# Turning between two sets of accumulation banks, a postponed step and a moved weight sum in the second products of two MLPs

## The chip, the cores and the metric

The kernel runs on one core of a Trainium2 chip. The core has a matrix engine (TensorE, PE in the profile), a vector engine (VectorE, DVE), a scalar engine (ScalarE, ACT), a general engine (GpSimd, POOL) and a queue that issues transfers (SyncE, SP). Matrix products accumulate in eight banks of a memory called PSUM, and VectorE and ScalarE read them out. The metric is the time on the device in microseconds (us), the median of several runs.

## The reference

Two transformer layers on 1024 tokens of width 1024. Layer 0 mixes by sliding-window attention, layer 1 by a gated recurrence (HGRN2); each is followed by an MLP of inner width 4096, and a norm stands before each block and at the end.

```python
def sqrelu_mlp(h, w_up, w_down):
    return jnp.square(jax.nn.relu(h @ w_up)) @ w_down

for layer in range(DEPTH):
    h = rmsnorm(x, mix_norm[layer])
    y = attention(h) if layer % 2 == 0 else hgrn2(h)
    x = x + y
    h = rmsnorm(x, mlp_norm[layer])
    x = x + sqrelu_mlp(h, w_up[layer], w_down[layer])
return rmsnorm(x, final_norm)
```

The change is in the second product of the MLP, `squared @ w_down`: 1024 tokens x 4096 by 4096 x 1024, once in each layer.

## The kernel before

**Precision.** Every float32 operand of a large product is split into a rounded part and the rest (`split`, `weight_split`): a cast on ScalarE or VectorE makes the first (`wh` for weights), a subtraction on VectorE the second (`wl`). One 128x128x512 product is then three matmuls (`mm3`): high by high, high by low, low by high.

**Seven products in place of eight.** `down` cuts both operands into 2x2 blocks and forms the output from seven block products (the Strassen-Winograd scheme), numbered 1 to 7 as in `operands`. Each sums over 16 steps `p`; a step is 12 matmuls, four row blocks `m` times three, and so a product is 192 matmuls. "Pass 6" in this document is `run_pass((6,))`, the 16 steps of product 6; the first pass carries products 1 and 5 step by step together. `T[p]` holds running sums of activations and `S[p]` running sums of weights, both as tiles in on-chip memory; product 5 makes `S[p]`, product 6 uses it, and product 3 needs `a(0, 1) - S[p]`.

**Banks.** `main` is four PSUM banks (tag `q`) that collect products 1, 6, 7 and 4 one on top of another, and are copied out after each; `side` is four banks (tag `p`) for products 5, 2 and 3, each started afresh. The order of passes is (1, 5), 6, 7, 4, 2, 3. After (1, 5), 6 and 7 ScalarE copies `main` out, and after (1, 5) and 2 it copies `side`; after 4 VectorE reads `main` itself. Then VectorE adds block sums, multiplies by the token scale `r` and adds the residual (`scaled_sum`, on tiles that `residual` loads). A pass that writes the banks which the pass before it wrote must wait, bank by bank, for these copies.

**Operands.** `run_pass` emits the operands of step p + 2 ahead of the products of step p. `raw` loads a 256 KB weight tile (tag `wr`, five buffers), `hidden` loads a tile of activations (tag `t`); the split weights have five buffers each (`wh`, `wl`), the split activations come from the 60 buffers `a`. In pass 3 the last 4 steps of layer 0 and the last 8 of layer 1 are "held": their operands go into `a` tiles and their products are run later, interleaved with what follows (the start of HGRN in layer 0, the final norm in layer 1).

**What sets the order.** `Schedule` records all operations and then fixes the order of each engine's instructions by a list schedule: it goes forward with estimated costs, and gives each engine the ready operation of lowest rank, where rank is the place in the program (less a lead for weight loads and for reads of `p` banks). Casts may go to ScalarE or VectorE, whichever it reckons done earlier. Buffers are handed out in this estimated time. On the chip each engine runs its list strictly in order, so one late instruction holds up all that stand behind it. All loads and stores go through one SP queue, also in order.

Lines of `kernel.py` in the profile read L334 throughout, since every operation is issued from `Schedule`'s records; tiles tell them apart. The program prints here the functions that the change touches, and their callers.

Of the kernel before, what the change touches and what calls it, by code (L numbers as in the profile page):

```python
# [18 lines left out]
T = 1024  # L19
# [119 lines left out]
HK = KT // 2  # L139
# [140 lines left out]
class Net:  # L280
# [38 lines left out]
    def a(self, dt=F32, shape=(P, TH)):  # L319
        return self.tile("a", BUFS["a"], shape, dt)  # L320
# [455 lines left out]
    def operands(self, name, p, T, S, held=False):  # L776

        a = lambda i, k: self.raw(self.io["down"][self.layer, k, p, :, i])
        h = lambda i, hf: self.hidden(i, hf, p)

        def sum_of(tile, x, y, alu=ALU.subtract):
            self.tt("any", tile, x, y, alu)
            return tile

        if name == 1:
            self.corner = a(0, 0), h(0, 0)
            w, x = self.corner
        elif name == 5:
            first, q00 = self.corner
            T[p] = x = sum_of(self.a(), h(0, 1), q00)  # L790
            w = sum_of(self.t(tag="m"), a(1, 0), a(1, 1), ALU.add)
        elif name == 6:
            T[p] = x = sum_of(T[p], h(1, 1), T[p])
            w = S[p]
        elif name == 7:
            x = sum_of(self.t(), h(1, 1), h(0, 1))
            w = sum_of(self.t(tag="m"), a(0, 0), a(1, 0))
        elif name == 4:
            x = sum_of(T[p], h(1, 0), T[p])
            w = a(1, 1)  # L800
        elif name == 2:
            w, x = a(0, 1), h(1, 0)
        else:
            x = h(1, 1)
            w = sum_of(S[p], a(0, 1), S[p])
        got = self.split(w) if held else self.weight_split(w), self.split(x)
        if name == 5:
            S[p] = sum_of(self.a(), w, first)
        return got

    def down(self, cut):

        n, ahead = MT // 2, 2
        T, S, y = {}, {}, {}
        main = [self.psum("q") for _ in range(HK)]
        side = [self.psum() for m in range(HK)]

        def products(names, ps, ws, start, stop, tokens=slice(0, TH), ms=range(HK)):
            for p in ps:
                for name in names:
                    (wh, wl), (xh, xl) = ws[name, p]
                    for m in ms:
                        out = (main if name in (1, 6, 7, 4) else side)[m][:, tokens]
                        c = slice(m * P, m * P + P)
                        more = {"skip_group_check": True} if name in (6, 7, 4) or not start else {}
                        first = p == 0 and not more
                        self.mm3(out, (wh[:, c], wl[:, c]), (xh[:, tokens], xl[:, tokens]), first, p == stop,  # L830
                                 tokens.stop - tokens.start, **more)

        def run_pass(names, held=0):
            ws, todo = {}, list(range(n))
            for p in range(n):
                while todo and todo[0] <= p + ahead or (todo and todo[0] >= n - held and p >= n - held - 1):
                    q = todo.pop(0)
                    for name in names:
                        ws[name, q] = self.operands(name, q, T, S, q >= n - held)
                if p < n - held:  # L840
                    products(names, [p], ws, True, n - held - 1)
            return ws

        def scaled_sum(hf, out, z, tokens=slice(0, TH)):

            k = tokens.stop - tokens.start
            u = self.t(tag="m")[:, :k]
            self.tt("DVE", u, z, self.r[hf][:, tokens], ALU.mult, k)
            part = out[:, tokens].only(tokens.start)
            self.tt("any", part, u, part, ALU.add, k)  # L850

        def residual(m, hf):
            z = self.a()
            self.dma(z, self.x[m][hf], 4 * P * TH)
            return z

        run_pass((1, 5))
        for m in range(HK):
            y[0, 0, m], y[1, 1, m] = self.a(), self.a()
            self.copy(y[0, 0, m], main[m])  # L860
        for m in range(HK):
            self.copy(y[1, 1, m], side[m])
        run_pass((6,))
        for m in range(HK):
            u = y[0, 1, m] = self.a()
            self.copy(u, main[m])
        for m in range(HK):
            self.tt("DVE", y[0, 1, m], y[0, 1, m], y[1, 1, m], ALU.add)
        run_pass((7,))
        parts = [self.t() for _ in range(HK)]  # L870
        for m in range(HK):
            self.copy(parts[m], main[m])
        for m in range(HK):
            self.tt("DVE", y[1, 1, m], parts[m], y[1, 1, m], ALU.add)
        for i in range(2):
            for m in range(HK):
                z = residual(m + (1 - i) * HK, 1)
                scaled_sum(1, z, y[1 - i, 1, m])
                self.x[m + (1 - i) * HK][1] = z
        run_pass((4,))  # L880
        for m in range(HK):
            z = residual(m + HK, 0)
            scaled_sum(0, z, main[m])
            self.x[m + HK][0] = z
        run_pass((2,))
        parts = [self.t() for _ in range(HK)]
        for m in range(HK):
            self.copy(parts[m], side[m])
        for m in range(HK):
            self.tt("DVE", y[0, 0, m], parts[m], y[0, 0, m], ALU.add)  # L890
            z = residual(m, 0)
            scaled_sum(0, z, y[0, 0, m])
            self.x[m][0] = z
        if not cut:
            held = 4
            ws = run_pass((3,), held)
            yield 0, slice(0, TH)
            for m in range(HK):
                products((3,), range(n - held, n), ws, False, n - 1, ms=[m])
                scaled_sum(1, self.x[m][1], side[m])  # L900
            yield 1, slice(0, TH)
            return
        held = n // 2
        ws = run_pass((3,), held)
        yield 0, slice(0, TH)
        for c in (0, TH // 2):
            tokens = slice(c, c + TH // 2)
            for m in range(HK):
                products((3,), range(n - held, n), ws, False, n - 1, tokens, [m])
                scaled_sum(1, self.x[m][1], side[m][:, tokens], tokens)  # L910
            yield 1, tokens
# [629 lines left out]
```

## Time and profile before

| | |
|---|---|
| median of 3 runs | 2154.43 us (2151.45, 2154.43, 2158.83) |
| profiled execution | 2151.11 us, span 2149.3 us |
| TensorE busy | 2114.5 us, 98% of the span |
| VectorE busy | 1866.9 us, 87% |
| ScalarE busy | 993.3 us, 46% |
| mean granted TensorE clock | 0.996 |
| moved by DMA | 333.91 MB, 155 GB/s in the mean |

The second product of layer 0 runs from about 632 to 949 us of the span and that of layer 1 from about 1813 to 2138 us. Rows of groups give line, engine, operation, the tile written and the tiles read (`q<-a,wh`), their shapes, the count, then busy time and the mean of one in ns, and after the second bar the idle time of the engine just before them and what ended it. Rows of time give the start and the length in us and, in brackets, idle time before. Rows of windows give, for a stretch of the span, the busy time and the number of instructions of each engine, then the granted clock of TensorE, the share of time in which the DMA engines were busy, and GB/s. An idle row of an engine that is not the slowest costs nothing by itself; TensorE's does.

### The profile page before, as it was taken

The page shows a single profiled execution, that of the slowest core. Times are in us where ns is not written, and L with a number is a line of the kernel's source. Part 1 is how long each engine was busy: PE and PEld are TensorE (multiplying, and loading weights), DVE is VectorE, ACT ScalarE, POOL GpSimd, SP SyncE. Part 2 cuts the span into 40 slices and gives each one's busy share as a digit, 9 for nine tenths or more (in the row PEclk, how much of TensorE's full clock was granted, in tenths as well). Part 3 has the DMA queues.
Part 4 walks back from the last instruction along what each step waited for, and adds up shares of the span by engine and source line. Part 5 has one row for each costly group of instructions (what it writes and reads, how often), then busy time and mean ns, then how long its engine had stood idle before and what let it go on. Part 6 is the DMA issues. An engine that isn't in the chain of part 4 may idle for free.

```text
span 2149.3 us, 33980 instructions
## 1 busy us (share of the span) xinstructions
PE 2114.5 (98%) x11968; PEld 1734.0 (81%) x11968; DVE 1866.9 (87%) x3822; ACT 993.3 (46%) x2031; POOL 61.7 (3%) x121
## 2 busy tenths in 40 slices
PE   9999999999999999999999999999999999999998
PEld 7778777888888887877788888788788888888787
DVE  8889899888899988899888888878988889899886
ACT  5567777444454234465333333343644445423444
POOL 4020000000000000000100000000000000000000
PEclk9999999999999999999999999999999999999999
DMA  6212275443468876731111111547444446897652
GB/s 214 77 50 83 80 245 167 131 134 124 137 197 293 299 248 219 255 111 55 59 60 55 60 55 60 189 155 227 165 133 133 128 132 202 282 301 244 200 177 79
DMA packets 183787, 333.91 MB, mean 155 GB/s; under 512 B 20672, under 2 KB 22720, under 8 KB 183616
## 3 DMA queue, kind: packets, MB, share of 16 engines
q1 hardware_dynamic: 183616, 331.74, 47.3%
q8 instruction: 94, 1.54, 0.3%
q14 instruction: 77, 0.63, 0.1%
HBM read 265.60 MB, written 66.06 MB: 154 GB/s over the span
## 4 chain that ended last, share of the span: by engine, by line
PE 54%; issue 36%; DVE 5%; ACT 3%; DMA 1%; SPq 0%; POOL 0%; POOLq 0%; ACTq 0%; DVEq 0%
PE p L334 29%; PE q L334 25%; DVE a L334 2%; DVE t L334 2%; ACT a L334 1%; ACT t L334 1%; DVE wl L334 1%; DVE m L334 1%; DMA t<-d 0%; ACT wh L334 0%; DVE wh L334 0%; DMA wr<-in_up 0%; DVE sm L334 0%; DMA a<-in_x 0%; DMA d<-t 0%
## 5 line engine op out<-in xcount | busy, mean ns | idle before, releaser
L334 PE MATMUL p<-a,wh 128*128 128x512 f32 (+1 forms) x2616 | 775.0, 378 | 5.8 <-ACT wh L334 4.0
L334 PE MATMUL q<-a,wh 128*128 128x512 f32 x2336 | 734.9, 396 | 6.8 <-ACT t L334 5.0
L334 PEld LDWEIGHTS p<-a,wh 128*128 128x128 f32 x2616 | 469.3, 188 | 96.5 <-ACT wh L334 5.0
L334 PEld LDWEIGHTS q<-a,wh 128*128 128x128 f32 x2336 | 432.1, 189 | 102.6 <-ACT t L334 7.5
L334 PE MATMUL p<-a,wl 128*128 128x512 f32 (+1 forms) x1308 | 488.5, 374 | 1.8 <-DVE wl L334 1.7
L334 PE MATMUL q<-a,wl 128*128 128x512 f32 x1168 | 460.9, 395 | 0.3 <-DVE wl L334 0.3
L334 PEld LDWEIGHTS p<-a,wl 128*128 128x128 f32 x1308 | 246.3, 188 | 46.9 <-DVE wl L334 2.7
L334 PEld LDWEIGHTS q<-a,wl 128*128 128x128 f32 x1168 | 220.1, 188 | 52.7 <-DVE wl L334 0.8
L334 DVE TENSOR_TENSOR wl<-wr,wh 128x512 fp32r<-128x512 f32 x352 | 241.2, 687 | 15.6 <-ACT wh L334 5.3
L334 ACT ACTIVATE t<-t 128x512 f32<-128x512 f32 x238 | 148.1, 631 | 169.8 <-DVE t L334 163.5
L334 DVE TENSOR_TENSOR wl<-m,wh 128x512 fp32r<-128x512 f32 x312 | 212.5, 687 | 5.1 <-ACT wh L334 0.4
L334 DVE TENSOR_TENSOR a<-t,a 128x512 fp32r<-128x512 f32 (+2 forms) x304 | 199.1, 677 | 3.4 <-DMA t<-d 2.9
L334 ACT COPY t<-q 128x512 f32<-128x512 f32 (+2 forms) x201 | 111.1, 559 | 193.0 <-PE q L334 171.7
L334 ACT CAST a<-t 128x512 fp32r<-128x512 f32 (+1 forms) x203 | 121.5, 611 | 144.1 <-PE q L334 73.9
L334 ACT CAST wh<-wr 128x512 fp32r<-128x512 f32 x180 | 111.1, 620 | 162.8 <-PE p L334 93.0
L334 DVE TENSOR_TENSOR t<-t,t 128x512 f32<-128x512 f32 (+3 forms) x299 | 173.6, 599 | 12.2 <-DMA t<-d 6.2
L334 ACT CAST wh<-m 128x512 fp32r<-128x512 f32 x200 | 123.5, 622 | 128.6 <-PE p L334 66.1
L334 DVE CAST wh<-wr 128x512 fp32r<-128x512 f32 x172 | 73.5, 428 | 118.2 <-PE q L334 78.5
L334 DVE TENSOR_TENSOR m<-wr,wr 128x512 f32<-128x512 f32 (+1 forms) x188 | 119.3, 647 | 18.8 <-DMA wr<-in_down 16.1
L334 PE MATMUL p<-wh,a 128*128 128x512 f32 x384 | 126.0, 399 | 0.5 <-ACT a L334 0.4
L334 PEld LDWEIGHTS q<-t,t 128*64 128x64 f32 (+1 forms) x2160 | 98.0, 144 | 25.0 <-issue 10.9
L334 PE MATMUL q<-t,t 128*64 128x32 f32 (+2 forms) x2160 | 111.5, 230 | 0.0
(125 smaller groups left out, 2323.7 us busy)
## 6 DMA issues: line engine op xcount, KB each, us to landing
t<-d SPq DMA_DIRECT2D x312, 256.0 KB, 4.7
wr<-in_down SPq DMA_DIRECT2D x256, 256.0 KB, 4.1
d<-t SPq DMA_DIRECT2D x188, 256.0 KB, 3.1
wr<-in_up SPq DMA_DIRECT2D x170, 256.0 KB, 3.1
wr<-in_win SPq DMA_DIRECT2D x68, 256.0 KB, 2.8
a<-d SPq DMA_DIRECT2D x60, 256.0 KB, 4.4
wr<-in_wqkv SPq DMA_DIRECT2D x48, 256.0 KB, 2.9
d<-a SPq DMA_DIRECT2D x48, 256.0 KB, 3.4
```

The lines of the kernel that those rows point to most:

```text
L334: fn(*[place(a) for a in args], **{k: place(v) for k, v in kw.items()})
```

## The change

Three edits in `operands` and `down`, for both layers:

1. **Order of passes.** (1, 5), 6, 7, 2, 4, 3 in place of (1, 5), 6, 7, 4, 2, 3. From pass 6 on, the banks written alternate: `main`, (`side` for one step), `main`, `side`, `main`, `side`.
2. **Part of product 5 put off.** Step 15 of product 5 is taken out of the first pass and run by itself after pass 6. Its split weight goes to `a` tiles (`held` is true for it) in place of `wh` and `wl`. The copies of `side` into `y[1, 1, m]` follow it, after pass 6 in place of before.
3. **Weight sums of product 3.** `S[p] = a(0, 1) - S[p]` is made in pass 2, from the weight tile which pass 2 has loaded; pass 3 takes `S[p]` and does not load `a(0, 1)` again: 16 loads of 256 KB fewer in each layer.

```diff
@@ operands
         elif name == 2:
             w, x = a(0, 1), h(1, 0)
+            S[p] = sum_of(S[p], w, S[p])
         else:
-            x = h(1, 1)
-            w = sum_of(S[p], a(0, 1), S[p])
+            w, x = S[p], h(1, 1)
@@ down
-        def run_pass(names, held=0):
+        def run_pass(names, held=0, kept=()):
             ws, todo = {}, list(range(n))
             for p in range(n):
                 while todo and todo[0] <= p + ahead or (todo and todo[0] >= n - held and p >= n - held - 1):
                     q = todo.pop(0)
                     for name in names:
-                        ws[name, q] = self.operands(name, q, T, S, q >= n - held)
+                        ws[name, q] = self.operands(name, q, T, S, q >= n - held or (name, q) in kept)
                 if p < n - held:
-                    products(names, [p], ws, True, n - held - 1)
+                    products([name for name in names if (name, p) not in kept], [p], ws, True, n - held - 1)
             return ws
...
-        run_pass((1, 5))
+        ws = run_pass((1, 5), kept=[(5, n - 1)])
         for m in range(HK):
-            y[0, 0, m], y[1, 1, m] = self.a(), self.a()
+            y[0, 0, m] = self.a()
             self.copy(y[0, 0, m], main[m])
-        for m in range(HK):
-            self.copy(y[1, 1, m], side[m])
         run_pass((6,))
+        products((5,), [n - 1], ws, True, n - 1)
         for m in range(HK):
             u = y[0, 1, m] = self.a()
             self.copy(u, main[m])
+        for m in range(HK):
+            y[1, 1, m] = self.a()
+            self.copy(y[1, 1, m], side[m])
...
-        run_pass((4,))
-        for m in range(HK):
-            z = residual(m + HK, 0)
-            scaled_sum(0, z, main[m])
-            self.x[m + HK][0] = z
         run_pass((2,))
         parts = [self.t() for _ in range(HK)]
...
             scaled_sum(0, z, y[0, 0, m])
             self.x[m][0] = z
+        run_pass((4,))
+        for m in range(HK):
+            z = residual(m + HK, 0)
+            scaled_sum(0, z, main[m])
+            self.x[m + HK][0] = z
```

## The prediction

> **What bounds the kernel now.** I read the page first, then the waits of TensorE, then windows cut at the passes, then the timeline at the two places where TensorE stood still.
>
> ```profile
> span 2149.3 us, 33980 instructions
> PE 2114.5 (98%) x11968; PEld 1734.0 (81%) x11968; DVE 1866.9 (87%) x3822; ACT 993.3 (46%) x2031; POOL 61.7 (3%) x121
> ```
> ```profile
> PE q L334 <- ACT t L334: 6.9, 6, 2.3
> PE p L334 <- ACT wh L334: 4.0, 1, 4.0
> ```
>
> TensorE is the bound; no matmul is removed, so only its idle time (2149.3 - 2114.5 = 34.8 us, start and end included) and time at a lowered clock can be won. The two largest waits lie in `down`: a wait for copies of a `q` bank (`t<-q`) and one for a weight cast. The windows show each in its pass. The first four rows are passes 7, 4, 2 and 3 of layer 0, the last three 7, 4 and 2 of layer 1.
>
> ```profile
> core 0: us, PE busy (x) PEld busy (x) DVE busy (x) ACT busy (x) POOL busy (x), PEclk, DMA share, GB/s
> 769.80:815.20 45.40, 44.63 (x193) 35.86 (x191) 41.90 (x72) 16.07 (x30) 0.00 (x0) 1.00 0.86 289
> 815.20:859.90 44.70, 44.66 (x193) 36.17 (x194) 36.41 (x63) 17.45 (x31) 0.00 (x0) 1.00 0.67 209
> 859.90:904.40 44.50, 44.50 (x194) 36.04 (x193) 35.76 (x63) 15.95 (x28) 0.00 (x0) 1.00 0.77 249
> 904.40:949.40 45.00, 40.98 (x175) 32.98 (x174) 41.32 (x100) 29.15 (x54) 0.36 (x2) 0.96 0.50 164
> 1951.10:1998.00 46.90, 44.61 (x193) 35.87 (x191) 43.02 (x74) 16.07 (x30) 0.00 (x0) 1.00 0.89 298
> 1998.00:2044.00 46.00, 45.99 (x192) 37.34 (x193) 36.62 (x63) 17.21 (x31) 0.00 (x0) 0.96 0.58 180
> 2044.00:2088.60 44.60, 44.60 (x194) 36.05 (x193) 36.89 (x64) 17.51 (x31) 0.00 (x0) 1.00 0.64 204
> ```
>
> An undisturbed pass of 192 matmuls takes 44.5 to 44.6 us, 0.232 us a matmul. Passes 7 and 4 together cost 90.1 us in layer 0 and 92.9 in layer 1, against 89.2 undisturbed: 0.9 and 3.7 us too long. Pass 3 of layer 0 has 45.0 - 40.98 = 4.0 us of idle TensorE.
>
> **Where the turn from pass 7 to pass 4 stalls.** Both write `main`. First layer 0, then layer 1:
>
> ```profile
> 806.47 1.36 DVE L334 TENSOR_TENSOR a<-m,a 128x512 f32<-128x512 f32 x2 [1.99 <-DMA a<-d]
> 814.09 0.62 ACT L334 CAST a<-a 128x512 fp32r<-128x512 f32 x1 [0.86 <-DVE a L334]
> 814.61 1.56 ACT L334 COPY t<-q 128x512 f32<-128x512 f32 x3
> 815.24 0.73 PE L334 MATMUL q<-a,wh 128*128 128x512 f32 x2 [0.82 <-ACT t L334]
> ```
> ```profile
> 1988.94 0.70 DVE L334 TENSOR_TENSOR a<-m,a 128x512 f32<-128x512 f32 x1 [1.38 <-DMA a<-d]
> 1996.85 0.62 ACT L334 CAST a<-a 128x512 fp32r<-128x512 f32 x1 [0.86 <-DVE a L334]
> 1997.38 1.55 ACT L334 COPY t<-q 128x512 f32<-128x512 f32 x3
> 1998.01 1.22 PE L334 MATMUL q<-a,wh 128*128 128x512 f32 x2 [2.30 <-ACT t L334]
> ```
>
> The copies of the banks are late because they stand in ScalarE's queue behind casts, these wait for VectorE, and VectorE had waited 2.0 (1.4) us for a residual tile. The matmul waits for nothing else: it starts 0.63 us after the copies begin. Layer 1 pays twice, since the clock drops behind the wait, as it does behind the wait in pass 3 of layer 0:
>
> ```profile
> 925.20:928.60 3.40, 3.34 (x10) 2.65 (x11) 3.40 (x8) 1.21 (x3) 0.00 (x0) 0.65 0.00 0
> 928.60:932.00 3.40, 3.40 (x14) 2.75 (x13) 3.40 (x14) 3.40 (x7) 0.00 (x0) 0.85 0.08 23
> 1998.00:2001.40 3.40, 3.39 (x8) 2.72 (x9) 3.40 (x7) 3.05 (x6) 0.00 (x0) 0.50 0.61 173
> ```
>
> At half the clock for 3.4 us, 1.7 us are lost. [...]
>
> **Where pass 3 of layer 0 stalls.**
>
> ```profile
> 922.00 1.64 ACT L334 CAST wh<-a 128x512 fp32r<-128x512 f32 x3
> 924.61 0.60 ACT L334 CAST wh<-a 128x512 fp32r<-128x512 f32 x1
> 925.26 0.96 PE L334 MATMUL p<-a,wh 128*128 128x512 f32 x3 [4.02 <-ACT wh L334]
> ```
>
> The matmul of step 6 waits for the cast at 924.61. By the order of the program's instructions, ScalarE makes the casts of steps 8, 7, 9 and 10 ahead of that of step 6, and that of step 10 needs a buffer which the second-last matmul of step 5 releases. So the order itself forbids step 6 to follow step 5 at once: a release, then four ScalarE instructions.
>
> **The change, part by part.**
>
> *New order of passes.* After it pass 7 (`main`) is followed by pass 2 (`side`, last read after pass 6), pass 2 by 4 (`main`, last read after 7) and 4 by 3 (`side`, read after 2). No first matmul of these waits for a copy that is younger than a whole pass: the bank waits at 815.24 and 1998.01 go. Gain: 0.9 us in layer 0, 3.7 in layer 1. What is late next is VectorE, since its wait for the residual tile stays. In the changed program's order the first sum that waits for a residual is followed by 28 VectorE instructions up to `wl` of step 4 of the new pass 2, the tightest operand that I find.
>
> ```profile
> 815.51 1.89 DVE L334 TENSOR_TENSOR a<-t,a 128x512 f32<-128x512 f32 x3
> ```
>
> Back to back one takes (1.89 - 0.68) / 2 = 0.605 us. Started at 806.47 and 1988.94 as before, 29 of them end at 824.0 and 2006.5. Unstalled, pass 7 would end at 814.4 and 1995.7 (44.6 us after it began) and the matmul in question, the 51st of its pass, start 11.6 us later: 826.0 and 2007.3. Slack 2.0 and 0.8 us, thin but there. It should be more, since only 5 of the 16 weight sums stand ahead of the residual sums, where the old pass 7 made all 16 activation sums of pass 4 ahead of them: 11 fewer, 6.7 us. I take 0; the bound above is the old waits again, 0.9 and 3.7 us.
>
> *Pass 1 to 6, step 15 of product 5 put off.* This turn is now the only one from `main` to `main`: the 12 matmuls of product 5 that covered it move behind pass 6, where they cover the turn to 7. The copies there as they ran:
>
> ```profile
> 720.57 1.98 ACT L334 COPY a<-q 128x512 f32<-128x512 f32 x3 [0.30 <-PE q L334]
> 722.44 0.62 ACT L334 CAST a<-a 128x512 fp32r<-128x512 f32 x1
> 722.96 0.59 ACT L334 COPY a<-q 128x512 f32<-128x512 f32 x1
> ```
>
> Bank 0 is free at 721.2 and the last of step 15's own matmuls ends about 722.5: ScalarE itself waits for each bank here, and writes come 2.1 us (nine matmuls) after a bank's last one. Cost 0; the bound above is a wait as in the old turns, 0.8 to 2.3 us and 1.7 for the clock. The operands of pass 6 are wanted 2.8 us (12 matmuls) sooner; VectorE makes the first `wl` of pass 6 in the same place of its queue as it made that of step 15. The four copies of `side` and four sums of VectorE that need them go from pass 6 to the start of pass 7: 4 x 0.6 us on each, and behind them VectorE has operands that are wanted 12 us later. Cost 0.
>
> *Weight sums into pass 2.* 16 subtractions a layer move from pass 3 (in the old program they were mostly made early, in pass 2). 32 loads fewer on SP; the tiles of step 5 on stand behind the eight residual loads there, as in the old pass 4. POOL's list is unchanged. The old pass 4 had the same work of VectorE as the new pass 2 gets (16 sums, 32 splits and the 12 operations after product 7), in 36.4 of 44.7 us. The new tie is that a sum waits for its weight tile, five or six instructions behind the release that lets SP load it. How the same sums ran in the old pass 2:
>
> ```profile
> L334 DVE TENSOR_TENSOR a<-wr,a 128x512 f32<-128x512 f32 x14 | 9.5, 686 | 1.3 <-DMA wr<-in_down 1.2
> ```
>
> Cost 0, between 0 and the 8.3 us of free VectorE time used up. The loads dropped were hidden: gain 0.
>
> *Pass 3 of layer 0.* Its stall goes by the new order: the cast of step 6 now stands three places behind that of step 7, and nothing ahead of it waits for a matmul later than the 37th before the one that it feeds (8.6 us). ScalarE also loses the four bank copies at the start of pass 3, because product 4 is read by VectorE. Gain 4.0 + 1.7 = 5.7 us; between 0, if ScalarE stays as full as it was, and 5.7. VectorE has to come along by 6.6 us in layer 0. Its waits from pass 4 to the end of pass 3:
>
> ```profile
> DVE wh L334 <- PE q L334: 7.4, 8, 1.0
> DVE wh L334 <- PE p L334: 6.7, 7, 1.6
> DVE sm L334 <- PE q L334: 1.6, 1, 1.6
> ```
>
> It waited 15.7 us for TensorE there, and still 1.6 us at the last point, where the next norm begins. So I let the gain through. Pass 3 of layer 1 has no stall to win.
>
> Sum: 0.9 + 3.7 + 5.7 = 10.3 us off the profiled execution's 2151.1, 2140.8. That execution lies at the lowest of the three runs; against the median of 2154.4 the same sum gives 2144.1. The runs spread by 7 us, so about 0.3% is what a measurement of this kernel can tell from no change.
>
> **Rivals.**
>
> *VectorE becomes the wait in the new pass 2* (its thin slack fails, the old stall comes back as one for `wl`). For it: 0.8 us of slack in layer 1 at the old lateness. Against: 11 sums fewer ahead. Only 5.7 us are won: 2148.7.
>
> *The 5.7 us of pass 3 aren't won*, because the cast stays late or because the start of HGRN is bound by VectorE:
>
> ```profile
> 950.00:1000.00 50.00, 48.89 (x223) 38.74 (x221) 48.99 (x86) 30.88 (x56) 0.00 (x0) 1.00 0.17 58
> ```
>
> It is 98% busy there. Against: its wait of 1.6 us just before. Then 4.6 us: 2149.8.
>
> *Nothing changes, since copies were hidden anyway.* Against: two waits for `t<-q` with their clock. For: the turns from 6 to 7 and from 2 to 3 have no wait in the same trace. 2154. [...]
>
> *Slower: weight tiles come late for the sums.* In the new pass 2 SP loads each tile only when VectorE has released its buffer, and VectorE's next sum stands five or six instructions (3.0 to 3.6 us) behind. If each of the 16 then waited 1.2 us, 19.2 us would meet 8.3 free: 10.9 us a layer, 21.8 less 10.3 won, 2165.9. It makes the change a loss from (8.3 + 5.2) / 16 = 0.84 us a sum. Against it: 1.3 us for 14 sums above.
>
> **How the numbers follow.** The forecast 0.74; VectorE in pass 2 0.07; pass 3 not won 0.09; nothing 0.02; slower 0.08. The likeliest is 2144.1. Downward, the sum off the lowest run gives 2140.8, and another 2 us for lesser waits 2139. Upward the range takes in the rivals to 2152 and leaves out the loss and part of the no change. Faster by over 0.3% (below 2148.0) is the forecast alone: 0.74; within: 0.07 + 0.09 + 0.02 = 0.18; slower 0.08.
>
> **What would show it.** Right: passes 7 and 2 of the new order 44.6 us each in both layers, no `q` wait for `t` in `down`, clock 1.00 through pass 4; pass 3 of layer 0 without a wait for `wh`; pass 1 to 6 without a wait. Wrong: TensorE waits for `wl` early in pass 2, VectorE waits for `wr<-in_down` above some 8 us a layer, a new `q` wait for `a` where pass 6 begins, or more TensorE waits between 930 and 1060 us.

## The result and the profile after

The changed kernel takes 2141.19 us in the median of six runs (2138.13 to 2142.52), the kernel before 2153.54 us in six runs beside them (2148.07 to 2158.83). The ratio is 0.9943, with a 95% interval of 0.993 to 0.9955: 12.3 us, or 0.57%, faster. The profiled execution took 2142.52 us, the longest of the six, and so lies only 8.6 us below that of before (2151.11 us). First its page, span and busy times, then the view of waits, the two largest of TensorE in the whole run:

```profile
span 2140.7 us, 33915 instructions
PE 2112.7 (99%) x11968; PEld 1735.4 (81%) x11968; DVE 1867.1 (87%) x3826; ACT 991.3 (46%) x2027; POOL 60.6 (3%) x121
```
```profile
PE q L334 <- ACT t L334: 4.1, 5, 1.8
PE p L334 <- DVE wl L334: 2.8, 5, 1.7
```

The bank wait of 2.3 us and the cast wait of 4.0 us are gone; TensorE has 28.0 us outside its busy time where it had 34.8. The windows of the changed kernel, cut at its passes: first 7, 2, 4 and 3 of layer 0 (the last one 45 us long, as before), then 7, 2 and 4 of layer 1. Columns are those of the windows of before.

```profile
772.80:817.50 44.70, 44.70 (x194) 36.06 (x193) 39.30 (x70) 11.86 (x22) 0.00 (x0) 1.00 0.73 228
817.50:861.85 44.35, 44.35 (x194) 36.04 (x193) 43.81 (x75) 20.33 (x38) 0.00 (x0) 1.00 0.81 268
861.85:906.35 44.50, 44.50 (x193) 36.06 (x192) 41.58 (x74) 22.54 (x41) 0.36 (x2) 1.00 0.63 214
906.35:951.35 45.00, 45.00 (x200) 36.67 (x199) 40.09 (x97) 23.21 (x42) 0.00 (x0) 1.00 0.45 147
1946.65:1991.10 44.45, 44.45 (x194) 36.05 (x193) 39.87 (x71) 11.80 (x21) 0.00 (x0) 1.00 0.73 227
1991.10:2035.55 44.45, 44.45 (x193) 36.05 (x192) 44.35 (x75) 20.42 (x37) 0.00 (x0) 1.00 0.79 259
2035.55:2080.05 44.50, 44.50 (x194) 36.06 (x193) 38.44 (x69) 22.19 (x41) 0.00 (x0) 1.00 0.36 120
```

TensorE is busy for the whole of each, at the full clock; no wait of it is listed between 640 and 960 us or between 1815 and 2125 us. Set side by side by the first matmul of each pass, the two traces differ so: the first pass of layer 0, counted in both without step 15 of product 5, is 0.6 us shorter, 7 and its successor 1.05 us, pass 3 up to its step 12 5.84 us (39.23 to 33.39); in layer 1, 7 and its successor 4.03 us (92.94 to 88.91), the rest 0.1. Together some 11.7 us are won inside `down`; the 0.6 us of the first pass are not the change's, since that pass is as short in two kernels with the old order below (87.7 us in place of 88.3). The two profiled executions differ by 3 us less because the part ahead of it, which the change leaves alone, took 3.7 us longer in the later one; what that was is the last section's matter.

### The profile page after: what moved, and what is told of

Read it like the earlier page. It is cut to its first block, busy times and chain, and to the rows that moved or that the text cites. A ratio compares the mean times of both kernels' runs of the same rounds, so it can differ in the third digit from the quotient of the medians.

```text
span 2140.7 us, 33915 instructions
## 1 busy us (share of the span) xinstructions
PE 2112.7 (99%) x11968; PEld 1735.4 (81%) x11968; DVE 1867.1 (87%) x3826; ACT 991.3 (46%) x2027; POOL 60.6 (3%) x121
## 4 chain that ended last, share of the span: by engine, by line
PE 88%; DVE 6%; ACT 2%; DMA 2%; issue 1%; SPq 0%; POOLq 0%; POOL 0%; DVEq 0%; ACTq 0%
PE q L334 45%; PE p L334 43%; DVE t L334 2%; DVE a L334 2%; DVE wl L334 1%; ACT a L334 1%; DVE m L334 1%; ACT t L334 1%; DMA a<-in_x 1%; DMA d<-t 1%; DMA t<-d 0%; DVE wh L334 0%; ACT wh L334 0%; DMA wr<-in_win 0%; SPq L334 0%
## 5 line engine op out<-in xcount | busy, mean ns | idle before, releaser
L334 ACT CAST wh<-wr 128x512 fp32r<-128x512 f32 x194 | 119.7, 619 | 170.6 <-PE p L334 102.7
L334 DVE TENSOR_TENSOR t<-t,t 128x512 f32<-128x512 f32 (+4 forms) x299 | 173.6, 598 | 12.2 <-DMA t<-d 6.8
L334 ACT CAST wh<-m 128x512 fp32r<-128x512 f32 x186 | 114.7, 622 | 107.9 <-PE p L334 61.9
L334 DVE CAST wh<-wr 128x512 fp32r<-128x512 f32 x158 | 67.4, 427 | 99.0 <-PE q L334 69.8
L334 PEld LDWEIGHTS q<-t,t 128*64 128x64 f32 (+1 forms) x2160 | 98.0, 144 | 25.0 <-issue 10.9
```

Of the source, the lines that this page charges most:

```text
L334: fn(*[place(a) for a in args], **{k: place(v) for k, v in kw.items()})
```

## The experiments

**One edit alone, and two together.** The first question is which of the three edits carries the gain. My theory was that the order of the passes carries all of it; the rival that the other two are needed for the turns or for pass 3. The kernel before with the new order alone (order_only):

```diff
-        run_pass((4,))
-        for m in range(HK):
-            z = residual(m + HK, 0)
-            scaled_sum(0, z, main[m])
-            self.x[m + HK][0] = z
         run_pass((2,))
...
+        run_pass((4,))
+        for m in range(HK):
+            z = residual(m + HK, 0)
+            scaled_sum(0, z, main[m])
+            self.x[m + HK][0] = z
```

> Only the new order of passes (2 ahead of 4); step 15 of product 5 stays in the first pass and the weight sums stay in pass 3. Theory (the order carries the whole gain): no wait at the turn from 7 to the next pass in either layer, no wait for `wh` in pass 3 of layer 0, ratio 0.994 to 0.996, as with all three edits; from the first matmul of `down` to the start of HGRN 7 to 8 us less than before, in layer 1 4 us less. Rival (the other edits are needed): a turn from 6 to 7 that waits for the copies, 1 to 4 us in each layer, or the stall of pass 3 stays at 4 us; ratio 0.996 to 0.999.

Measured: 2140.26 us in the median, ratio 0.9942 (0.9919 to 0.9964). From the first matmul of the first pass to the HGRN matmul at which the stretches further below end it takes 330.2 us (635.84 to 966.02) where before took 337.3 (634.10 to 971.37), and in layer 1 4.6 us less; no wait of TensorE is listed in either `down`. The rival falls: one edit of the three gives the whole gain.

The kernel before with the weight sums in pass 2 alone (sums_only):

```diff
         elif name == 2:
             w, x = a(0, 1), h(1, 0)
+            S[p] = sum_of(S[p], w, S[p])
         else:
-            x = h(1, 1)
-            w = sum_of(S[p], a(0, 1), S[p])
+            w, x = S[p], h(1, 1)
```

> Only the weight sums moved into pass 2, old order of passes. Theory: nothing of the gain; in the order of the instructions the cast of step 6 in pass 3 of layer 0 still stands behind one that waits for the second-last matmul of step 5, so the wait for `wh` of 4 us is still there, and the turn from 7 to 4 waits 0.8 us in layer 0 and about 2 us in layer 1; ratio 0.999 to 1.001. Rival (pass 3 stalled since VectorE and ScalarE were full there, and the sums relieve it): the 4 us are gone, ratio 0.997.

And with the step put off alone (step_only; `run_pass` takes `kept` as in the whole change):

```diff
-        run_pass((1, 5))
+        ws = run_pass((1, 5), kept=[(5, n - 1)])
         for m in range(HK):
-            y[0, 0, m], y[1, 1, m] = self.a(), self.a()
+            y[0, 0, m] = self.a()
             self.copy(y[0, 0, m], main[m])
-        for m in range(HK):
-            self.copy(y[1, 1, m], side[m])
         run_pass((6,))
+        products((5,), [n - 1], ws, True, n - 1)
         for m in range(HK):
             u = y[0, 1, m] = self.a()
             self.copy(u, main[m])
+        for m in range(HK):
+            y[1, 1, m] = self.a()
+            self.copy(y[1, 1, m], side[m])
```

> Only step 15 of product 5 put off, old order of passes. Theory: nothing, since the turn from 6 to 7 had no wait before and the turn from 1 to 6 has none without its cover; all three stalls stay; ratio 0.999 to 1.001. Rival: the uncovered turn from 1 to 6 waits 0.8 to 2.3 us in each layer, ratio 1.001 to 1.003.

Measured: 0.9991 (0.9974 to 1.0007) and 0.9997 (0.9984 to 1.0009). Both still have the stall of pass 3; TensorE's longest wait for a cast, in the sums alone and then in the step alone:

```profile
PE p L334 <- ACT wh L334: 2.4, 1, 2.4
```
```profile
PE p L334 <- ACT wh L334: 3.4, 2, 3.3
```

Neither edit changes the time by itself beyond the noise, and so the step put off costs nothing either. The turn from 7 to 4 of layer 1 waited 0.9 us here and 1.6 us there, against 2.3 in the profile of before: a stall whose size changes from one execution to the next.

Then the first two of these diffs together (order_sums), which is the change without the step put off:

> New order and weight sums, step 15 of product 5 not put off. Theory: the same time as with all three edits (ratio 0.994 to 0.996) and no wait at the turn from 6 to 7; VectorE's lead in pass 6 of layer 0 is about 3 us, not 0.5. Rival: the turn from 6 to 7 now waits for the copies, 1 to 4 us in each layer, ratio 0.996 to 0.998.

Measured: 2140.47 us, 0.9944 (0.9922 to 0.9966). The turn from 6 to 7, again on the same banks, has no wait. VectorE's lead in pass 6 was 1.7 us, not 3.

**Each cause by itself, in the old order.** Next the two stalls are mended without touching order or banks. In cast_only the weight casts of pass 3 in layer 0 go to ScalarE alone (`weight_split` hands `engines` to its `copy`):

```diff
+        engines = ("ACT",) if name == 3 and self.layer == 0 else ("ACT", "DVE")
-        got = self.split(w) if held else self.weight_split(w), self.split(x)
+        got = self.split(w) if held else self.weight_split(w, engines), self.split(x)
```

> The kernel before, but in pass 3 of layer 0 the weight casts may go to ScalarE alone; by the order of its instructions the cast of step 6 then stands in its turn, ahead of those of steps 7 to 10. Banks, passes and sums as before. Theory (the stall of pass 3 was an accident of the list of casts): the wait of 4 us for `wh` is gone, from the start of pass 3 to step 12 it takes 33.4 us in place of 39.2 (37.6 and 39.6 in the two runs with the old order), ratio 0.997 to 0.998. Rival (ScalarE is too full there while it copies the banks of pass 2): a wait of 2 us or more for a cast or for `wl` stays in pass 3, ratio above 0.9985.

Measured: the wait in pass 3 is gone, and pass 3 takes 33.4 us up to step 12, as expected; yet the ratio is 0.9991 (0.9979 to 1.0002). The gain is given back at the start of HGRN. Its trace there:

```profile
971.10 0.69 DVE L334 TENSOR_TENSOR m<-wr,m 128x512 f32<-128x512 f32 x1
971.70 1.89 DVE L334 TENSOR_TENSOR a<-t,a 128x512 fp32r<-128x512 f32 x3
972.18 0.61 ACT L334 CAST wh<-m 128x512 fp32r<-128x512 f32 x1
972.84 0.74 PE L334 MATMUL p<-a,wh 128*128 128x512 f32 x2 [3.18 <-ACT wh L334]
974.25 0.79 PE L334 MATMUL p<-a,wl 128*128 128x512 f32 x1 [0.67 <-DVE wl L334]
```

The matmul waits for a cast of a weight sum that VectorE made late; with the second wait and a half clock behind it (the matmul at 974.25 takes 0.79 us, its like in order_only below, at 967.16, 0.50), 3.18 + 0.67 + 1.7 = 5.6 us of the 5.8 are lost again; the 1.7 is an estimate, 3.4 us at half the clock as in the rows of before.

In residual_early four residual tiles are loaded ahead of pass 7:

```diff
+        early = {(1, m): residual(m, 1) for m in range(HK)}
         run_pass((7,))
...
-                z = residual(m + (1 - i) * HK, 1)
+                z = early.get((i, m)) or residual(m + (1 - i) * HK, 1)
```

> The kernel before, but the four residual tiles that the first sums after pass 7 read are loaded ahead of pass 7. Theory (the turn from 7 to 4 stalled only because VectorE waited for a residual tile, and ScalarE's casts and then its copies for VectorE): no wait at this turn in either layer although `main` follows `main`; passes 7 and 4 take 89.1 us together in both layers, in place of 90.1 and 92.9; the stall of pass 3 stays; ratio 0.9975 to 0.9995. Rival (a turn on the same banks costs by itself): 0.4 us or more of wait stay at the turn in each layer, ratio 0.9990 to 1.000.

Measured: 0.9986 (0.9973 to 0.9998). Its windows of passes 7 and 4, layer 0 and then layer 1, and the copies of the banks at the turn of layer 0 (the first matmul of pass 4 starts at 816.81):

```profile
772.30:816.80 44.50, 44.50 (x193) 36.05 (x192) 42.55 (x75) 17.31 (x32) 0.00 (x0) 1.00 0.86 290
816.80:861.35 44.55, 44.55 (x193) 36.06 (x192) 37.37 (x65) 16.20 (x30) 0.00 (x0) 1.00 0.66 211
1952.20:1996.85 44.65, 44.65 (x194) 36.04 (x193) 42.24 (x74) 17.34 (x32) 0.00 (x0) 1.00 0.86 286
1996.85:2041.45 44.60, 44.60 (x193) 36.03 (x192) 37.22 (x65) 16.17 (x30) 0.00 (x0) 1.00 0.61 186
```
```profile
814.93 1.98 ACT L334 COPY t<-q 128x512 f32<-128x512 f32 x3 [0.29 <-PE q L334]
```

ScalarE now waits for the banks and not they for it. The turn on the same banks cost nothing here (44.50 to 44.65 us a pass, TensorE busy for the whole of it), since the copies were not late; what had made them late was VectorE's wait for a residual tile, as predicted.

Both of these edits together (both_old_banks):

> Both of these edits, still with the old order of passes and banks. Theory: nothing is left in `down` that the new order could win; the time is that of the change, ratio 0.994 to 0.9965, and TensorE waits nowhere between 640 and 950 us and between 1830 and 2120 us. Rival: a turn on the same banks keeps a cost that only the alternation removes, 2 us or more above the change, ratio 0.996 to 0.998.

Measured: 2146.15 us, 0.9974 (0.9965 to 0.9984). There is no wait within the passes, but 3.1 and 0.7 us at the start of HGRN, as in cast_only. My expectation was wrong: the new order does more than keep the turns and the casts right. The ratio lies where the rival put it, but not for the rival's reason, since no turn on the same banks waits.

**What lets the gain through.** The stretch from the start of pass 3 in layer 0 to the HGRN matmul that waited, in four kernels. VectorE's busy time and count are the third pair after the comma. Before:

```profile
904.40:971.37 66.97, 62.67 (x271) 50.38 (x270) 62.96 (x136) 45.35 (x84) 0.36 (x2) 0.97 0.38 128
```

cast_only:

```profile
908.80:972.84 64.04, 60.87 (x271) 49.30 (x269) 62.65 (x136) 47.00 (x87) 0.36 (x2) 1.00 0.38 128
```

order_only:

```profile
904.36:966.02 61.66, 60.72 (x271) 49.28 (x269) 58.62 (x129) 40.64 (x73) 0.36 (x2) 1.00 0.39 129
```

The changed kernel:

```profile
906.36:967.41 61.05, 60.83 (x271) 49.29 (x269) 56.15 (x124) 37.10 (x68) 0.00 (x0) 1.00 0.35 117
```

TensorE's own work in it is 60.9 us. In the old order VectorE has 62.7 to 63.0 us to do there, more than TensorE; in the new order 58.6, since what follows pass 2 (copies, block sums and residuals) now runs in the pass ahead of this stretch, in which VectorE is busy for 41.4 us in place of 35.8. A kernel between the two tests this, cast_only with the diff of sums_only (cast_and_sums):

> Old order of passes and banks, with the casts of pass 3 of layer 0 in their turn and the weight sums made in pass 2. With the casts alone, VectorE was busy for 62.65 of the 64.04 us from the start of pass 3 to the matmul of HGRN that waited 3.18 us for it; TensorE's own work there is 60.86 us. The sums take some 2.4 us of VectorE's work out of that stretch (58.6 in the new order without them, 56.2 with). Theory (VectorE's work in this stretch sets when HGRN can start, not banks or casts): 60.3 us of VectorE's work, the wait at the start of HGRN falls from 3.2 us to between 0.3 and 1.2, no half clock there; from pass 3 to that matmul 61.2 to 62.2 us; ratio 0.996 to 0.998. Rival (that wait is of the old order itself, a load or a bank): it stays at about 3 us.

```profile
904.39:965.56 61.17, 60.89 (x272) 49.30 (x270) 59.77 (x131) 44.71 (x83) 0.36 (x2) 1.00 0.34 117
```

VectorE's work is 59.8 us, below TensorE's, and the wait falls from 3.18 to 0.28 us, with 0.20 behind it and no half clock there (the matmul at 966.50 takes 0.50 us), as the theory has it. (The sums also take 2.3 us from ScalarE here, 47.0 to 44.7, and the list of instructions is made anew with each edit; no run parts these.) The sum of VectorE's work is not the whole of it either. In order_only it is smaller, 58.6 us, and yet TensorE waits longer at the same place, while VectorE stood still for a weight tile of HGRN:

```profile
966.02 0.73 PE L334 MATMUL p<-a,wh 128*128 128x512 f32 x2 [0.94 <-ACT t L334]
967.16 0.50 PE L334 MATMUL p<-a,wl 128*128 128x512 f32 x1 [0.41 <-DVE wl L334]
```
```profile
DVE m L334 <- DMA wr<-in_win: 2.2, 1, 2.2
```

The ratio of cast_and_sums is 0.9982 (0.9968 to 0.9996), 2148.2 us in the median, though the profiled run took 2143.3, almost the fastest of ten; the traces do not show where its slower runs lose 5 to 9 us.

The opposite test loads the changed kernel behind the residuals of pass 4 (vector_load):

```diff
+        for _ in range(11 if not cut else 0):
+            self.tt("DVE", T[n - 1], T[n - 1], T[n - 1], ALU.subtract)
```

> The changed kernel with 11 idle subtractions (6.7 us of VectorE's work) put behind the last activation of pass 4 in layer 0. Theory (the new order wins at the start of HGRN because it takes 6.5 us of VectorE's work out of the stretch from the start of pass 3): VectorE is busy for about 62.8 us in it, the wait at the start of HGRN is back at 2.5 to 3.5 us with, by the place of the grid, 1.7 us for the clock, and no wait appears in pass 3; 2143.5 to 2147.5 us. Rival (VectorE has slack there, as its waits of 15.7 us in the trace of before suggested): no new wait over 0.5 us, 2140 to 2143 us.

The grid of this expectation is that of the last section. Measured: 2137.75 us in its one run, and a wait of 0.26 us. The load did not go where it was meant to:

```profile
903.07:964.19 61.12, 60.86 (x271) 49.30 (x269) 56.39 (x124) 37.00 (x68) 0.00 (x0) 1.00 0.34 117
```

VectorE has 56.4 us in the stretch, as without the load. The list put the subtractions beside pass 4 (VectorE 43.7 us there in place of 41.6) and gave ScalarE seven more instructions there (48 for 41). So this run says nothing on the stretch, and the amount of VectorE's work there stays without a test from this side; it says that 6.7 us more beside pass 4 are taken in without loss, 2.1 of them by VectorE and the rest by casts that go over to ScalarE.

**VectorE's lead at the turn from 1 to 6.** In the changed kernel the last operand of step 2 of pass 6 in layer 0 was ready 0.5 us ahead of its matmul. Two kernels add 2.4 us of VectorE's work in front of it, in `run_pass` at step 0 of pass 6 of layer 0: lead_after to the changed kernel, lead_order_sums to order_sums.

```diff
+    z, junk = T[2][:, :P], self.const((P, P))
+    for _ in range(12):
+        self.tt("DVE", junk, z, z, ALU.subtract, P)
```

> The changed kernel with 12 idle subtractions of 128 columns (about 2.4 us of VectorE's work) at the end of the first pass of layer 0. VectorE's lead over TensorE is thinnest at step 2 of pass 6 there, 0.5 us. Theory (the lead is real time of VectorE, and what is added comes out of it): TensorE waits 1.5 to 2.3 us in all for `wl` or `a` at the start of pass 6 of layer 0, and nowhere else. Rival (VectorE runs far enough ahead in the first pass and takes them in its own waits): no wait there.

> The same 12 subtractions in the kernel with the new order and the weight sums, but step 15 of product 5 not put off. The lead at the same place was 1.7 us. Theory (putting off the step costs lead there and wins nothing): TensorE waits 0.3 to 1.2 us less there than with the step put off. Rival (the step put off keeps banks apart and so saves a wait that shows only under load): it waits as long or longer, and at the turn from 6 to 7 as well.

Neither waits at the turn, and both take 2139 us, in one run each. The window of the first pass and VectorE's longest wait in it, in the changed kernel and then in lead_after:

```profile
637.78:725.51 87.73, 87.73 (x386) 71.20 (x385) 79.08 (x133) 40.29 (x74) 0.00 (x0) 1.00 0.89 287
```
```profile
DVE m L334 <- DMA wr<-in_down: 7.6, 7, 2.0
```
```profile
636.33:724.05 87.72, 87.72 (x387) 71.20 (x385) 80.86 (x143) 41.84 (x77) 0.00 (x0) 1.00 0.90 295
```
```profile
DVE m L334 <- DMA wr<-in_down: 6.5, 6, 1.8
```

VectorE waits 7.6 us for weight tiles there; of the 1.8 us by which it is busier in lead_after, 1.1 come out of such waits. The thin lead of 0.5 us, behind an engine that itself waits for loads, was no sign that it is full. The rival I had named holds, and on the step put off the pair tells nothing.

**When the clock drops.**

The last kernel puts pauses into TensorE (gaps_by_size), to see whether the length of a wait parts those behind which the clock drops from the others. `dead` and `due` are activations of steps p and p + 1: VectorE may write the first only when step p has read it, and step p + 1 must wait for the copy of the second onto itself.

```diff
+SIZES = (256, 768, 1280, 512, 1536, 1024, 640, 896, 1152)
...
+    def bubble(self, dead, due):
+        self.bubbles = getattr(self, "bubbles", -1) + 1
+        left, z = SIZES[self.bubbles % len(SIZES)], dead.bitcast(F32)
+        while left > 0:
+            k = min(left, TH)
+            self.tt("DVE", dead[:, :k], z[:, :k], z[:, :k], ALU.subtract, k)
+            left -= k
+        z = due[:, :P]
+        self.op("DVE", self.nc.vector.tensor_copy, [due], [due, dead], 140, z, z.bitcast(F32))
...
+                    if names[0] in (6, 7, 2, 4) and p in (3, 6, 9, 12):
+                        self.bubble(ws[names[0], p][1][1], ws[names[0], p + 1][1][1])
```

> The changed kernel with 32 pauses put into TensorE: in passes 6, 7, 2 and 4 of both layers, at steps 3, 6, 9 and 12, VectorE does 256 to 1536 columns of idle subtraction behind the end of the step, and the next step waits for it, so that the waits are about 1 to 2.6 us long. [...]

The run took 2218.07 us, with a mean granted clock of 0.985 where the changed kernel's profiled execution had 0.995, and the pauses came out at up to 7.5 us, since VectorE fell behind. One of them, with the three stretches of 3.41 us around it (the granted clock is the third number from the end):

```profile
853.25 0.50 PE L335 MATMUL p<-a,wh 128*128 128x512 f32 x1 [2.77 <-DVE a L335]
```
```profile
848.08:851.49 3.41, 2.39 (x11) 1.62 (x9) 3.41 (x6) 1.18 (x2) 0.00 (x0) 1.00 0.77 220
851.49:854.90 3.41, 1.65 (x7) 1.39 (x8) 3.41 (x8) 0.00 (x0) 0.00 (x0) 1.00 0.90 312
854.90:858.32 3.42, 3.42 (x17) 2.80 (x16) 3.42 (x7) 1.51 (x3) 0.00 (x0) 1.00 0.89 277
```

A wait of 2.77 us, of which 1.02 us lie in the first of these stretches and 1.76 in the second, leaves the clock at 1.00. In the trace of before the clock was 0.50 behind the wait of 2.30 us that ended at 1998.01, and in that of the changed kernel behind one of 1.55 us (at 85.62, last section). So in these traces the length of the wait does not decide: the longest of the three left the full clock and the two shorter ones did not.

## Why the prediction was right, and where it was not

**Order of passes, turn from 7.** Right in cause and in size: 0.9 and 3.7 us were named, 1.05 and 4.03 measured between the two traces, no bank wait left. But the reason given for the gain (no matmul waits for a young copy) is only one way to it; residual_early wins the same turn on the same banks. And the 3.7 us came from one execution: passes 7 and 4 of layer 1 took 92.9 us in it, but 90.2, 91.1 and 89.5 in sums_only, step_only and cast_only, against 88.9 undisturbed. One trace priced a stall of 0.6 to 4.0 us at its upper end.

**VectorE in the new pass 2.** The lead at `wl` of step 4 was put at 2.0 and 0.8 us or more. In layer 0 that `wl` and the activation's rest of the same step, and the matmul that reads `wl`:

```profile
825.71 0.68 DVE L334 TENSOR_TENSOR wl<-wr,wh 128x512 fp32r<-128x512 f32 x1
826.31 0.68 DVE L334 TENSOR_TENSOR a<-t,a 128x512 fp32r<-128x512 f32 x1
```
```profile
829.09 0.39 PE L334 MATMUL p<-a,wl 128*128 128x512 f32 x1
```

It is 829.09 - 826.39 = 2.7 us (3.8 in layer 1). The tightest operand was the other one, ready at 826.99 for a matmul at 828.86: 1.9 us (2.9 in layer 1). The term of 0 and the refusal of that rival were right.

**Pass 1 to 6.** Cost 0, right, with the 2.8 us of lead lost as worked out (3.3 to 0.5 us). VectorE, on which this lead rests, was paced by weight tiles, which the prediction did not see.

**Weight sums.** Cost 0, right. VectorE's waits for weight tiles in the changed kernel's `down` of layer 0:

```profile
DVE m L334 <- DMA wr<-in_down: 8.3, 9, 2.0
...
DVE a L334 <- DMA wr<-in_down: 1.8, 4, 0.6
```

The 16 sums are the second row: 0.11 us each, far from the 0.84 at which the loss would have begun. The sign that I gave for a wrong forecast (above some 8 us a layer) did fire, at 10.1 us, and meant nothing: it counted the sums of products 5 and 7 as well, which are the first row.

**Pass 3 of layer 0.** 5.7 us named, 5.84 measured, and the cause (the cast out of its turn) is shown by cast_only, where that alone removes the wait.

**The step that failed** is the one behind it: "So I let the gain through", because VectorE "waited 15.7 us for TensorE there, and still 1.6 us at the last point". That sum runs over three passes. In the trace of before, 7.4 us of it lie in pass 4 and 6.7 in pass 2, ahead of casts into `wh`: VectorE waits there until TensorE frees one of the five buffers, and the time is gone when pass 3 starts. From there on only the 1.6 us are left, and these come behind TensorE's own stand of 4.0 us. In cast_only, from the start of pass 2 to where TensorE stops at 969.66 us, the waits for `wh` are there as before and the 1.6 us are not:

```profile
DVE wh L334 <- PE p L334: 6.9, 7, 1.6
DVE m L334 <- DMA wr<-in_win: 0.9, 1, 0.9
DVE a L334 <- DMA wr<-in_down: 0.7, 2, 0.4
DVE m L334 <- PE p L334: 0.4, 1, 0.4
```

So there was no room where the prediction saw it. The stall goes, VectorE's 62.7 us no longer fit into TensorE's 60.9, and 5.6 of 5.8 us come back as a wait at HGRN, which is the prediction's own second rival. In the changed kernel the gain came through most likely because the order of passes takes 4.0 us of VectorE's work out of this stretch (62.65 to 58.62), and 6.5 with the sums (56.15), which the prediction did not count; ScalarE's work there falls too (47.0 to 40.6 and 37.1), and no run parts the two. The outcome was right, its reason wrong, and so this term came right by luck.

**The sum.** 10.3 us against 10.9 measured for the same terms (1.05 + 4.03 + 5.84). The median came 2.9 us below the 2144.1 forecast: 0.6 us of it is this difference, 0.9 the median of before, which six runs put at 2153.5, and the rest lies within the interval of the ratio, which is 5 us wide. That the sum fits so well is in part luck too, since its second term, 3.7 us, came out at 0.6 to 4.0 by the trace that one takes.

## What to carry to other kernels

Compare the work of the next engine with the undisturbed work of the bounding one over the same stretch, from where the stall goes to the next point where they meet. What the next engine waits for free buffers ahead of that stretch, or while the stall lasts, is no room in it. The turn on the same accumulation banks needed no second set in residual_early (44.50 and 44.55 us a pass), where the copies were on time: look first at what stands ahead of them in their queue. Price a stall from several executions, and test a change of several edits one by one: here moving one pass did all of it.

## What the runs showed of the hardware

In the trace of before the first three stretches at half clock (0.50) begin at 926.23, 1516.73 and 1998.01 us, each 3.41 us long; the steps between them are 173 and 141 times 3.4133 us. In the trace of the changed kernel such stretches begin at 86.96, 295.18, 1510.32 and 2131.55 us, with steps of 61, 356 and 182 times 3.4133 us; the first two are 3.41 us long, the third 6.83. So in each of the two the starts lie on one grid of time. Cut into cells of 3.41 us by these starts, the traces give this idle time of TensorE in a cell, and this clock in it and in the next:

| trace | cell from, us | idle TensorE, us | clock in it | clock in the next |
|---|---|---|---|---|
| before | 919.40 | 1.57 | 1.00 | 1.00 |
| before | 922.81 | 2.45 | 1.00 | 0.50 |
| before | 1513.32 | 2.64 | 1.00 | 0.50 |
| before | 1994.60 | 2.30 | 1.00 | 0.50 |
| changed | 83.55 | 1.64 | 1.00 | 0.50 |
| changed | 291.76 | 1.69 | 1.00 | 0.50 |
| changed | 1506.91 | 1.97 | 1.00 | 0.50 |
| changed | 1510.32 | 1.41 | 0.50 | 0.50 |
| changed | 1513.73 | 0.00 | 0.50 | 1.00 |
| changed, final norm | 2128.14 | 1.37 | 1.00 | 0.50 |

No one limit of idle time follows from this: 1.37 us in the final norm, among matmuls with a single column (128x1), were followed by the half clock and 1.57 us in pass 3 were not, and the 3.41 us with 1.76 us of idle time in gaps_by_size (851.49 to 854.90) had the full clock behind them. Why, no run tests.

The same wait cost differently in the two traces. Ahead of `down`, in a part which the change leaves alone, both kernels wait 1.55 us at the same matmul. Before, with three cells of its grid:

```profile
83.61 0.36 PE L334 MATMUL q<-a,a 128*128 128x256 f32 x1 [1.55 <-DVE a L334]
```
```profile
79.72:83.13 3.41, 2.34 (x13) 1.60 (x11) 1.43 (x4) 3.31 (x6) 0.00 (x0) 1.00 0.00 0
83.13:86.54 3.41, 2.53 (x11) 1.66 (x12) 3.19 (x8) 1.60 (x4) 0.00 (x0) 1.00 0.00 0
86.54:89.95 3.41, 3.41 (x20) 2.86 (x20) 3.28 (x7) 1.92 (x5) 0.00 (x0) 1.00 0.00 0
```

The changed kernel, with two cells of its own:

```profile
85.62 0.36 PE L334 MATMUL q<-a,a 128*128 128x256 f32 x1 [1.55 <-DVE a L334]
```
```profile
83.55:86.96 3.41, 1.77 (x10) 0.96 (x8) 2.23 (x6) 2.78 (x5) 0.00 (x0) 1.00 0.00 0
86.96:90.37 3.41, 3.41 (x12) 2.71 (x11) 3.25 (x6) 0.37 (x1) 0.00 (x0) 0.50 0.00 0
```

There the wait lies across two cells, with 1.07 and 0.88 us of idle time, and the clock stays at 1.00; here it falls into one cell, which has 1.64 us of idle time with its small gaps, and the next cell runs at 0.50. It happened once more at 295.18 us. Of the 3.7 us by which the changed kernel's profiled execution reached `down` later, 2.0 were there before the first of these stretches, from waits of 0.71 us at 9.51 and at 36.97 us and smaller ones; behind the first it was 2.5 us late, behind the second 3.7. The 1.7 us that the prediction put down to the clock in layer 1 come from one such stretch (1998.01 us, clock 0.50) in one execution, behind a wait of 2.30 us; in sums_only and step_only the same turn waited 0.9 and 1.6 us.
